# A two-layer hybrid decoder trunk on one core: low halves of weights by adding DMAs, value product with values stationary, last gate with tokens on partitions

## The chip, the core and the metric

The program runs on one core of one Trainium2 chip. A core has five engines that run side by side, each with its own queue of instructions in program order: TensorE (PE, matmuls; its weight loads are listed as PEld and overlap the matmuls), VectorE (DVE), ScalarE (ACT), GpSimd (POOL) and SyncE (SP), which here only issues DMAs. Sixteen DMA engines move data. Matmul results land in PSUM (eight banks of 128 partitions x 512 floats); everything else works in SBUF. The metric is the device time in microseconds of one execution, lower is better; it is the median of three runs.

## The reference

```python
h = x                                              # (1, 256, 1024)
for i in range(2):
    n = rmsnorm(h, norm_g[i])
    z = n @ w_in[i] + b_in[i]                      # 1024 -> 3652 columns
    (c_val, c_glu, c_gate, p_in, p_gate, q, k, v, a_gate, qi, ki, wi) = split(z)
    ya = conv_module(c_val, c_glu, ...) * silu(c_gate)          # 31 taps, layernorm, silu, 256x256
    yb = pool_mixer(p_in, ...) * silu(p_gate)                   # windows 2, 4, 8, 16
    q, k, qi, ki = rope(q), rope(k), rope(qi), rope(ki)
    # per query: the 64 best causal keys by the indexer's score, softmax over them, 8 heads of 64
    yc = sparse_attention(q, k, v, qi, ki, wi) * silu(a_gate)
    h = h + concat([ya, yb, yc]) @ w_out[i]        # 1024 x 1024
    h = h + (p[i] @ ple_w[i]) * sigmoid(h @ ple_gate_w[i])      # 256 x 1024, 1024 x 1024
return rmsnorm(h, final_norm_g)
```

## The kernel before, in words

All activations lie transposed: channels on partitions, the 256 tokens along the free axis (`h` is 128 x 8 x 256). Every large product is made of three products of rounded halves. A weight is cut into `hi`, its rounding to fp32r, and `lo` = weight - `hi`, an activation likewise (`xhi`, `xlo`, or `yhi`, `ylo`); `mm3` adds hi*xhi, hi*xlo and lo*xhi in PSUM, each a matmul of 128 x 128 weights with 256 columns. Small products (scores, value product, transposes) are plain fp32, which the trace lists as two matmul records each, transposes as one.

`chunk` brings in 1 MB of weights (128 x 2048) by a DMA from SP into one of three `raw` buffers and cuts it in two halves of 128 x 1024. For each, `copy` on ACT (L255) makes `hi`, and `sub_hi` makes `lo` on DVE (L275) or POOL (L277), whichever is free first in the recorded order. There are six `hi` and six `lo` buffers, so three chunks' worth. A half feeds 24 matmuls, a chunk 48.

A layer goes: norm factors; `gemm_in` for the projection in chunks of 256 columns (numbered, `C_VAL` = 0 to `QI` = 13), rotary by `rope_pair` with SBUF-to-SBUF DMAs (`zs<-z`) and multiplies on POOL or DVE; the indexer's scores and the choice of 64 keys (DVE); attention for query half t = 1, then 0; convolution, layernorm and pooling (mostly DVE and POOL, spread beside the projections); `gemm_out("out")`, residual add, `gemm_out("gate")`, sigmoid, multiply by `ple` = p @ ple_w, add. In the attention, `lg` (queries on partitions) is transposed to `pTs`, and the value product takes `pTs` as the stationary side and 64 columns of `vt` as the moving side, into `bank 7` with queries on partitions. The result is scaled by `rinv` into `oT` (tile `q4`) and later transposed back (`f,q` in the trace).

At the end of the second layer, `gemm_out("gate")` finishes the 8 column blocks in parts, the last two of one block each. Then come the sums of squares by matmuls with `ones` (`norm_scale`), the power -0.5 on POOL (`rsqrt`), two transposes that spread the factor over the partitions, and five multiplies on DVE, each followed by an output DMA.

The order is not that of the code. Every operation is recorded in `Order` with costs and dependencies, and `issue` writes all of them out, engine by engine, by rank: the length of the path behind an operation plus a number from the table `FIRST` for its tag. So the table decides what stands behind what on each engine.

Of the kernel before, what the change touches and what calls it, by code (L numbers as in the profile page):

```python
# [48 lines left out]
SP_FG = L * SP_N  # L49
SP_TOT = SP_FG + 8  # L50

RAW, HIL = 3, 6
WARM = 13
OUT_ORDER = (2, 3, 4, 5, 6, 7, 0, 1)
OUT_OUTER, GATE_OUTER = 6, 4

# [71 lines left out]
class Order:  # L128
# [83 lines left out]
    def mm(self, o, lhsT, rhs, start, stop):  # L212
        n, m = rhs.free_size(), lhsT.free_size()
        if rhs.dtype == F32:
            occ, flow = 2 * max(112 * m // 128, 833 * n // 1000 + 3), 1667 * n // 1000
            if lhsT.shape[0] <= 64:
                occ = 2 * max(112 * m // 128, 417 * n // 1000 + 3)
# [230 lines left out]
def trunk(ctx: ExitStack, tc: tile.TileContext, xT, pT, w_in, w_ki, w_v, w_out, w_gate, w_ple,  # L448
# [153 lines left out]
    def layer(l, sqs, ple):  # L602
# [360 lines left out]
        for d, n, o in acc:  # L963
            last = l == L - 1 and d == KT - 1
            r = slice(d, d + n)
            if d >= 6 and l == L - 1:
                sums.append(ring("g", 1, (128, 2, S))[:, d - 6:d - 5])
# [135 lines left out]
```

## Time and profile before

| what | value |
|---|---|
| median of three runs | 337.77 us (336.79 to 339.85) |
| the profiled execution | 337.35 us, of which the span from first to last instruction is 335.6 us |
| busy share PE, PEld, DVE, ACT, POOL | 94%, 91%, 78%, 55%, 34% |
| granted TensorE clock | full speed (2.4 GHz) from the warm-up until the tail |
| moved by DMA | 56.80 MB, mean 169 GB/s |

The busy share of PE is counted from overlapping matmuls, so it says little about spare room; the distance between the starts of neighbouring matmuls says more. The chain of the work that ended last belongs to PE for 54% of the span.

### The profile page before, as it was taken

How to read it: one execution, taken by the hardware profiler on the slowest of the kernel's cores; microseconds unless marked ns; L12 is line 12 of the kernel's file. 1: busy time of each engine (PE TensorE's matmuls, PEld its weight loads, DVE VectorE, ACT ScalarE, POOL GpSimd, SP SyncE). 2: the span in 40 equal slices, each digit the busy share in tenths (PEclk: the TensorE clock that was granted, in tenths of full speed). 3: DMA queues.
4: the chain of work that ended last, by engine and by line, in shares of the span. 5: the costliest groups of instructions: out<-in, count | busy, mean ns of one | idle time of the engine just before them, and what ended most of it. 6: DMA issues, size and time to landing. Idle time of an engine off the chain costs nothing.

```text
span 335.6 us, 6643 instructions
## 1 busy us (share of the span) xinstructions
PE 317.0 (94%) x2575; PEld 304.9 (91%) x2575; DVE 263.0 (78%) x566; ACT 185.0 (55%) x318; POOL 115.7 (34%) x106
## 2 busy tenths in 40 slices
PE   7799999889999999999999999989999999999991
PEld 3799999888899899999999999989889999999980
DVE  2987989899896847685696989999998962777573
ACT  3757553571657944565486635446775871647340
POOL 2004156588789600001101207697766000002000
PEclk9999999999999999999999999999999999999996
DMA  7997394532655082637237547275451641370003
GB/s 203 350 352 303 82 374 158 168 147 49 237 200 208 2 297 95 250 107 226 111 94 250 193 149 273 65 259 161 147 173 80 251 169 83 127 250 2 2 0 125
DMA packets 13406, 56.80 MB, mean 169 GB/s; under 512 B 2112, under 2 KB 3264, under 8 KB 7872
## 3 DMA queue, kind: packets, MB, share of 16 engines
q1 hardware_dynamic: 13088, 56.00, 47.8%
q8 instruction: 20, 0.33, 0.4%
q10 hardware_dynamic: 288, 0.39, 0.3%
q14 instruction: 10, 0.08, 0.1%
HBM read 51.93 MB, written 1.05 MB: 158 GB/s over the span
## 4 chain that ended last, share of the span: by engine, by line
PE 54%; DVE 14%; DMA 13%; ACT 8%; POOL 4%; issue 3%; SPq 2%; POOLq 0%; DVEq 0%; ACTq 0%
PE bank L221 51%; DMA raw<-in_w_in_dram 7%; DVE lo L275 4%; DMA zs<-z 4%; ACT hi L255 4%; PE bank L225 3%; SPq L307 2%; DMA raw<-in_w_ple_dram 2%; POOL zrk L267 2%; DVE bank L282 2%; DVE bank L265 1%; POOL zs L267 1%; ACT z L230 1%; ACT bank L230 1%; DVE xlo L275 1%
## 5 line engine op out<-in xcount | busy, mean ns | idle before, releaser
L221 PE MATMUL bank<-xhi,hi 128*128 128x256 f32 x528 | 150.8, 287 | 1.1 <-DVE f L282 0.6
L221 PE MATMUL bank<-xlo,hi 128*128 128x256 f32 (+1 forms) x528 | 147.3, 281 | 0.0
L221 PE MATMUL bank<-xhi,lo 128*128 128x256 f32 x512 | 143.9, 281 | 2.1 <-POOL lo L277 1.1
L255 ACT ACTIVATE hi<-raw 128x1024 fp32r<-128x1024 f32 (+2 forms) x95 | 93.9, 1015 | 61.0 <-PE bank L221 29.2
L275 DVE TENSOR_TENSOR lo<-raw,hi 128x1024 fp32r<-128x1024 f32 (+2 forms) x79 | 91.8, 1184 | 28.7 <-ACT hi L255 27.8
L221 PEld LDWEIGHTS bank<-xhi,hi 128*128 128x128 f32 x528 | 99.5, 189 | 2.6 <-DVE f L282 0.8
L221 PEld LDWEIGHTS bank<-xhi,lo 128*128 128x128 f32 x512 | 96.7, 189 | 2.7 <-DVE lo L275 1.4
L221 PEld LDWEIGHTS bank<-xlo,hi 128*128 128x128 f32 (+1 forms) x528 | 98.6, 187 | 0.1
L282 DVE SCALAR_TENSOR_TENSOR bank<-f,f,bank 128x256 f32<-128x256 f32 x116 | 56.0, 483 | 1.6
L277 POOL TENSOR_TENSOR lo<-raw,hi 128x1024 fp32r<-128x1024 f32 (+1 forms) x19 | 45.4, 2400 | 30.2 <-DVE lo L275 11.8
L221 PE MATMUL bank<-yhi,hi 128*128 128x256 f32 x128 | 36.2, 283 | 0.0
L221 PE MATMUL bank<-yhi,lo 128*128 128x256 f32 x128 | 35.9, 281 | 0.0
L221 PE MATMUL bank<-ylo,hi 128*128 128x256 f32 x128 | 35.9, 280 | 0.0
L277 POOL TENSOR_TENSOR xlo<-f,xhi 128x256 fp32r<-128x256 f32 x4 | 3.6, 924 | 73.2 <-ACT xhi L255 36.7
L221 PEld LDWEIGHTS bank<-yhi,hi 128*128 128x128 f32 x128 | 24.1, 188 | 0.1
L221 PEld LDWEIGHTS bank<-ylo,hi 128*128 128x128 f32 x128 | 24.1, 188 | 0.0
L221 PEld LDWEIGHTS bank<-yhi,lo 128*128 128x128 f32 x128 | 24.1, 188 | 0.0
L267 POOL TENSOR_TENSOR acc<-acc 128x256 f32<-128x256 f32 x3 | 2.2, 742 | 55.7 <-DVE acc L265 35.8
L265 DVE TENSOR_TENSOR bank<-bank,rb 128x512 f32<-128x512 f32 (+1 forms) x26 | 17.3, 672 | 3.8 <-PE bank L221 2.8
L221 PE MATMUL bank<-hi,xhi 128*128 128x260 f32 (+1 forms) x64 | 18.3, 286 | 0.0
L230 ACT ACTIVATE lg<-lg,nmax 128x256 f32<-128x256 f32 (+1 forms) x32 | 14.2, 448 | 7.1 <-DVE nmax L800 7.1
L221 PE MATMUL bank<-lo,xhi 128*128 128x260 f32 (+1 forms) x64 | 18.1, 283 | 0.0
(139 smaller groups left out, 480.3 us busy)
## 6 DMA issues: line engine op xcount, KB each, us to landing
raw<-in_w_in_dram SPq DMA_DIRECT2D x25, 1024.0 KB, 5.4
raw<-in_w_out_dram SPq DMA_DIRECT2D x8, 1024.0 KB, 4.8
raw<-in_w_gate_dram SPq DMA_DIRECT2D x8, 1024.0 KB, 4.8
zs<-z SPq DMA_DIRECT2D x40, 64.0 KB, 3.0
raw<-in_w_v_dram SPq DMA_DIRECT2D x2, 1040.0 KB, 5.6
raw<-in_w_ple_dram SPq DMA_DIRECT2D x8, 256.0 KB, 3.9
raw<-in_w_in_dram SPq DMA_DIRECT2D x4, 256.0 KB, 5.9
f<-in_xT_dram SPq DMA_DIRECT2D x4, 256.0 KB, 5.7
```

The lines of the kernel that those rows point to most:

```text
L221: lambda: self.nc.tensor.matmul(o, lhsT, rhs, start=start, stop=stop, skip_group_check=True))],
L225: self.add([("pe", 195, 109, None, lambda: self.nc.tensor.transpose(o, i, ident))], [i, ident], [o])
L230: self.add([self.on_act(o, i, lambda: self.nc.scalar.activation(o, i, func, bias=bias, scale=scale, **kw), len(ptr), self.TABLE.get(func), ...
L255: ways.append(self.on_act(o, i, lambda: self.nc.scalar.activation(o, i, AF.Copy)))
L265: ways.append(self.on_dve(n, lambda: self.nc.vector.tensor_tensor(o, a, b, op), late=late))
L267: ways.append(self.on_pool(n, lambda: self.nc.gpsimd.tensor_tensor(o, a, b, op)))
L275: ways.append(self.on_dve(n, lambda: self.nc.vector.tensor_tensor(o, a, hb, OP.subtract), late=late))
L277: ways.append(self.on_pool(n, lambda: self.nc.gpsimd.tensor_tensor(o, a, hb, OP.subtract)))
L282: self.add([self.on_dve(o.free_size(), lambda: self.nc.vector.scalar_tensor_tensor(o, a, s, b, op0=op0, op1=op1), len(ptr))], [a, b] + ptr ...
L307: self.add([("dma", nbytes, 590 if inner else 440, None, lambda: q.dma_start(o, i))], [i] if i.space != bass.MemoryType.DRAM else [], [o] ...
```

## The change

Four things change, and the table `FIRST` is another one throughout.

1. For seven of the projection's chunks (`SUMS`: Q1, K0, K1, V1, A0, A1, P_GATE), both halves, both layers, so 28 halves, `lo` is no longer a subtraction. ACT writes -`hi` into `lo` (`neg`), and a DMA issued by POOL adds `raw` to it in place (`plus`).
2. In the value product, `vt` (64 columns of one head) is stationary and `pTs` moves with 128 columns. The two heads of a pair write partitions 0 to 63 and 64 to 127 of bank 7, so the result is transposed already. The factors `rinv` are spread by ACT into a 128 x 512 tile `ons`, transposed four times, copied, and multiplied in. The later transposes of `oT` go.
3. In the last layer, the gate and ple products have tokens on partitions: the activations are stationary and the weights move with 512 columns (256 in the last two parts, see `LAST_PARTS`). `h` is transposed for it (`ht`, 16 transposes).
4. The final norm then works along the free axis: ACT squares with a sum (`ssq`), DVE folds the sums into `nv`, POOL takes the power, ACT and DVE scale. The final norm's weights come in as a 128 x 1024 tile `gb` (0.5 MB more to load). No matmul is left behind the last gate matmul. The output is written token by token.

```diff
+SUMS = {f"{a} {c} {l}" for a in range(2) for c in (Q1, K0, K1, V1, A0, A1, P_GATE) for l in range(L)}
+LAST_PARTS = ((0, 0, 512), (0, 512, 512), (1, 0, 512), (1, 512, 256), (1, 768, 256))
 FIRST = {
-    "at00 0": 144188, "at00 1": -27913, "at04 1": 2080, "at10 0": 181, "at10 1": -2016, "at12 0": 3776,
+    "at00 0": -341946, "at04 0": 78573, "at04 1": 97213, "at10 0": -120473, "at10 1": -75424, "at12 0": 24407,
...
+    def neg(self, o, i):
+        self.add([self.on_act(o, i, lambda: self.nc.scalar.activation(o, i.bitcast(F32), AF.Copy, scale=-1.0))], [i], [o])
+
+    def plus(self, o, i):
+
+        self.add([("pool", self.SUM_WAY, self.SUM_NEXT, None,
+                   lambda: self.nc.gpsimd.dma_start(o, i, accum_op=OP.add))], [i, o], [o])
...
                 with R.part(f"s{a // n} {tag}"):
+                    if f"{a // n} {tag}" in SUMS:
+                        R.copy(hi[:, :n], raw[:, a:a + n], "act")
+                        R.neg(lo[:, :n], hi[:, :n])
+                        R.plus(lo[:, :n], raw[:, a:a + n])
+                        continue
...
-                    for i in range(nh):
-                        hh = 2 * (g0 + i) + e
-                        for kt in range(t + 1):
-                            j = i * (t + 1) + kt
-                            R.mm(po[:, (c0 + i) * 64:(c0 + i + 1) * 64], pTs[:, j * 128:(j + 1) * 128],
-                                 vt[:, kt, hh * 64:(hh + 1) * 64], start=(g0 == 0 and e == 0 and j == 0), stop=(kt == t))
+                    held[e] = pTs
+                for i in range(nh):
+                    f = g0 + i
+                    for kt in range(t + 1):
+                        j = i * (t + 1) + kt
+                        for e in range(2):
+                            R.mm(po[64 * e:64 * e + 64, f * 128:(f + 1) * 128], vt[:, kt, (2 * f + e) * 64:(2 * f + e + 1) * 64],
+                                 held[e][:, j * 128:(j + 1) * 128], start=(f == 0 and kt == 0), stop=(kt == t))
...
+        for i, part in enumerate(order):
...
+                    xh, xl = hhi[:, k, t * 128:(t + 1) * 128], hlo[:, k, t * 128:(t + 1) * 128]
+                    with R.bundle():
+                        R.mm(o, xh, hi[:, c:c + n], start=(k == 0), stop=False)
+                        R.mm(o, xh, lo[:, c:c + n], start=False, stop=False)
+                        R.mm(o, xl, hi[:, c:c + n], start=False, stop=(k == KT - 1))
...
+            R.act(o, o, AF.Sigmoid)
+            R.tt(o, o, ple[:, t, r], OP.mult)
+            R.tt(ht[t][:, r], o, ht[t][:, r], OP.add)
...
+            R.act(junk[:, :n], ht[t][:, r], AF.Square, accum=ssq[:, t, nth:nth + 1])
+            R.tt(hg[t][:, r], ht[t][:, r], gb[:, r], OP.mult, "dve" if end else "dve pool")
...
+                R.stt(v, s1, 1.0 / D, v, OP.mult, OP.add)
+            if end:
+                y = ring(f"nyr{t}", 1, (128, 1))
+                R.pool(750, [v, mhalf], [y], lambda v=v, y=y: nc.gpsimd.tensor_tensor(y, v, mhalf[:, :1], OP.pow))
...
+                    R.scaled(o, o, y)
+                    R.dma(out[t * 128:(t + 1) * 128, c:c + n], o, n << 9, "sp" if q % 2 == 0 else "act")
```

How the instructions stand, at three places. The first is PE in the second layer's attention for t = 1, at the first value products; `vt,pTs` and `pTs,vt` are the value product, `f,lg` the transposes, `zrk,zrq` the scores. Before:

```order
L221 MATMUL bank7_68<-vt45_125,pTs59_139 128x64
L221 MATMUL bank4_65<-zrk54_134,zrq53_133 128x256 x2
L221 MATMUL bank5_66<-zrk54_134,zrq53_133 128x256 x2
L225 MATMUL bank6_67<-f0_69,lg12_92 128x128 x4
L221 MATMUL bank7_68<-vt45_125,pTs59_139 128x64 x3
```

And now, in the same layer:

```order
L226 MATMUL bank6_67<-f0_69,lg12_92 128x128 x4
L222 MATMUL bank7_68<-pTs59_139,vt45_125 64x128
L222 MATMUL bank4_65<-zrk54_134,zrq53_133 128x128 x4
L222 MATMUL bank7_68<-pTs60_140,vt45_125 64x128
L222 MATMUL bank7_68<-pTs59_139,vt45_125 64x128
L222 MATMUL bank7_68<-pTs60_140,vt45_125 64x128
L222 MATMUL bank7_68<-pTs59_139,vt45_125 64x128
L222 MATMUL bank7_68<-pTs60_140,vt45_125 64x128
L222 MATMUL bank7_68<-pTs59_139,vt45_125 64x128
L222 MATMUL bank7_68<-pTs60_140,vt45_125 64x128
```

The products of the two heads of a pair now alternate, in one run of seven and a single one ahead of it; there are six such runs and six single ones in the program.

The second place is POOL in the second layer, where the projections of keys, values and gates are under way; `zrq`, `zrk` and `zs` are rotary work, `lo` the low halves. Before:

```order
L267 TENSOR_TENSOR zrq53_133<-zrq53_133,zs39_119 128x512
L267 TENSOR_TENSOR zrk54_134<-zrk54_134,zs38_118 128x512
L277 TENSOR_TENSOR lo29_109<-raw16_96,hi19_99 128x1024
L267 TENSOR_TENSOR zrk54_134<-zrk54_134,zs39_119 128x512
L277 TENSOR_TENSOR lo26_106<-raw15_95,hi22_102 128x1024
L267 TENSOR_TENSOR pen052_132<-pen052_132,f4_79 128x128
L277 TENSOR_TENSOR lo27_107<-raw15_95,hi23_103 128x1024
```

And now:

```order
L287 DMA lo28_108<-raw16_96 128x1024
L287 DMA lo29_109<-raw16_96 128x1024
L268 TENSOR_TENSOR zrq53_133<-zrq53_133,zs39_119 128x512
L268 TENSOR_TENSOR zrk54_134<-z37_117,f4_79 128x512
L287 DMA lo24_104<-raw17_97 128x1024
L268 TENSOR_TENSOR zrk54_134<-zrk54_134,zs39_119 128x512
L278 TENSOR_TENSOR lo27_107<-raw15_95,hi23_103 128x1024
L268 TENSOR_TENSOR pen052_132<-pen052_132,f4_79 128x128
L287 DMA lo28_108<-raw16_96 128x1024
L287 DMA lo25_105<-raw17_97 128x1024
L287 DMA lo29_109<-raw16_96 128x1024
```

Adding DMAs stand between the rotary multiplies where subtractions stood, and there are more of them.

The third place is the end of PE's queue. Before, from the last gate matmul:

```order
L221 MATMUL bank_68<-xhi_114,lo_105 128x256
L221 MATMUL bank_65<-f_74,acc_111 128x1 x2
L221 MATMUL bank_65<-f_74,g_123 128x1 x4
L225 MATMUL bank_66<-f_69,nyr_121 128x128 x2
```

And now, from the last but one part of the gate:

```order
L222 MATMUL bank_63<-hi_101,xlo_115 128x256
L226 MATMUL bank_66<-f_69,f_80 128x128 x4
L226 MATMUL bank_62<-f_69,f_80 128x128 x4
L222 MATMUL bank_63<-hi_98,xhi_114 128x256
L222 MATMUL bank_63<-lo_108,xhi_114 128x256
L222 MATMUL bank_63<-hi_98,xlo_115 128x256
```

The sums and spreads behind the last gate matmul are gone; eight of the transposes of `h` stand ahead of the last part.

## Rows read from the trace of the kernel before

**Rows 1.** Stretches: length; busy PE, PEld, DVE, ACT, POOL; clock, DMA share, GB/s.
```profile
37.00:115.00 78.00, 74.63 (x610) 71.44 (x610) 68.50 (x192) 43.30 (x87) 53.60 (x43) 1.00 0.49 172
...
200.00:272.60 72.60, 70.64 (x581) 67.63 (x580) 67.66 (x184) 45.31 (x90) 43.57 (x38) 1.00 0.52 179
...
321.30:335.60 14.30, 6.45 (x50) 5.74 (x48) 7.69 (x19) 2.73 (x8) 1.44 (x2) 0.79 0.20 73
```

**Rows 2.** Chain that ended last, in order of time: start, length, what; one piece.
```profile
272.62 48.63 PE bank L221 x404
```

**Rows 3.** Waits of PE: who waited for whom; total us, times, longest.
```profile
PE bank L221 <- DVE lo L275: 1.4, 4, 0.5
...
PE bank L221 <- POOL lo L277: 1.1, 1, 1.1
```

**Rows 4.** Timeline of PE: start, length of the group, line, operands, count.
```profile
112.81 1.03 PE L221 MATMUL bank<-pd,mt 128*128 128x256 f32 x4
...
254.97 1.67 PE L221 MATMUL bank<-vt,pTs 128*128 128x64 f32 x14
256.48 0.61 PE L225 MATMUL bank<-f,lg 128*128 128x128 f32 x4
```

**Rows 5.** Weight loads by shape: busy us, mean ns; idle before.
```profile
L221 PEld LDWEIGHTS bank<-zrk,zrq 64*128 64x128 f32 x64 | 7.5, 186 | 3.7 <-POOL zrk L267 2.5 <-issue 0.2
...
L221 PEld LDWEIGHTS bank<-xlo,hi 128*64 128x64 f32 x16 | 2.1, 134 | 0.0
```

**Rows 6.** Timeline of PE around tiles of 64 columns and of 64 rows.
```profile
187.77 0.28 PE L221 MATMUL bank<-xlo,hi 128*64 128x256 f32 x1
187.88 0.28 PE L221 MATMUL bank<-xhi,hi 128*128 128x256 f32 x1
...
243.96 0.71 PE L221 MATMUL bank<-zrk,zrq 64*128 64x128 f32 x4
244.60 0.44 PE L225 MATMUL bank<-f,lg 128*128 128x128 f32 x2
```

**Rows 7.** Groups off PE: busy us, mean ns; idle before them and its ends.
```profile
L255 ACT ACTIVATE hi<-raw 128x1024 fp32r<-128x1024 f32 x82 | 84.3, 1055 | 50.7 <-PE bank L221 28.4 <-DMA raw<-in_w_in_dram 12.0 <-POOL qir L267 6.2
L275 DVE TENSOR_TENSOR lo<-raw,hi 128x1024 fp32r<-128x1024 f32 x64 | 79.2, 1262 | 22.2 <-ACT hi L255 21.4 <-PE bank L221 0.5
...
L277 POOL TENSOR_TENSOR lo<-raw,hi 128x1024 fp32r<-128x1024 f32 x18 | 44.1, 2461 | 23.2 <-DVE lo L275 11.8 <-ACT hi L255 8.5 <-DVE zrk L265 2.2
...
L230 ACT ACTIVATION_READ_ACCUMULATOR lg<-lg,nmax 128x1 f32 x32 | 6.1, 190 | 0.0
```

**Rows 8.** DMA: the main queue's share; issues, KB each, us to landing.
```profile
q1 hardware_dynamic: 13088, 56.00, 47.8%
...
raw<-in_w_in_dram SPq DMA_DIRECT2D x25, 1024.0 KB, 5.4
...
zs<-z SPq DMA_DIRECT2D x40, 64.0 KB, 3.0
```

**Rows 9.** Timeline of the tail, all engines.
```profile
323.95 0.36 ACT L230 ACTIVATE bank<-bank 128x256 f32<-128x256 f32 x1
...
324.69 0.43 DVE L265 TENSOR_TENSOR bank<-bank,ple 128x256 f32<-128x256 f32 x1
...
325.22 0.28 PE L221 MATMUL bank<-xhi,lo 128*128 128x256 f32 x1
...
325.86 0.42 ACT L248 ACTIVATE g<-f 128x256 f32<-128x256 f32 x1
...
326.88 0.35 DVE L294 TENSOR_SCALAR ag<-f,f 128x256 f32<-128x256 f32 x1
...
327.89 0.16 DVE L288 TENSOR_SCALAR nv<-bank 128x2 f32<-128x2 f32 x1 [0.65 <-PE bank L221]
328.13 0.70 POOL L547 TENSOR_TENSOR nyr<-nv,f 128x2 f32<-128x2 f32 x1 [2.54 <-DVE nv L288]
...
331.92 0.33 SPq L307 DMA_DIRECT2D out_dram<-ag  x1
```

More of the change, by code (lines that the diff above doesn't have):

```diff
@@ L325 @@
     VECTOR_PAUSE, POOL_LATE = 30, -500
+    SUM_WAY, SUM_NEXT = 5500, 1100
     def issue(self):
@@ L577, in ple_gemm @@
         w = chunk(f"ple {l}", w_ple[l], pieces=4, late=0 if l == 0 else VECTOR_LATE)
+        if l == L - 1:
+            ple = ring("ple", 1, (128, KT, S)).rearrange("p (t a) s -> p t (a s)", t=2)
+            for a in range(2):
+                hi, lo = (x[:, :1024].rearrange("p (b k n) -> p k b n", b=2, k=2) for x in w[a])
+                for t in range(2):
+                    pb = bank()
+                    o = pb.rearrange("p (b n) -> p b n", b=2)
+                    R.tag = f"g ple{2 * a + t} {l}"
+                    with R.grouped():
+                        for k in range(2):
+                            with R.bundle():
+                                c0 = k * S + t * 128
+                                xh, xl = phi[:, c0:c0 + 128], plo[:, c0:c0 + 128]
+                                R.mm(o, xh, hi[:, k], start=(k == 0), stop=False)
+                                R.mm(o, xh, lo[:, k], start=False, stop=False)
+                                R.mm(o, xl, hi[:, k], start=False, stop=(k == 1))
+                    R.copy(ple[:, t, a * 512:(a + 1) * 512], pb, "act dve")
+            return ple
         ple = ring("ple", 1, (128, KT, S))
@@ L960, in layer @@
             R.sub_hi(hlo[:, r, :], h[:, r, :], hhi[:, r, :], "dve pool")
+        if l == L - 1:
+            return last_gate(hhi, hlo, ple, [banks[3], bank("att"), bank("att"), bank()])
         acc = gemm_out("gate", w_gate, hhi, hlo)
-        sums = [ring("acc", 1, (128, 2, S))]
+        sums = ring("acc", 1, (128, 2, S))
         for d, n, o in acc:
-            last = l == L - 1 and d == KT - 1
             r = slice(d, d + n)
-            if d >= 6 and l == L - 1:
-                sums.append(ring("g", 1, (128, 2, S))[:, d - 6:d - 5])
-            for c in range(0, S, S // 2 if last else S):
-                t = slice(c, c + S // 2 if last else c + S)
-                R.tag = f"o{d} {l}"
-                s = o[:, :, t]
-                if last:
-                    if c == 0:
-                        sl = ring("lg", 2, (128, 512))
-                    s = sl[:, t].unsqueeze(1)
-                R.act(s, o[:, :, t], AF.Sigmoid)
-                R.tt(s, s, ple[:, r, t], OP.mult)
-                R.tt(h[:, r, t], s, h[:, r, t], OP.add)
-                R.tag = f"sq{d} {l}"
-                if d >= 6 and l == L - 1:
-                    R.sq(sums[-1][:, :, t], h[:, r, t])
-                elif d == 7:
-                    square(sums[0], 6)
-                elif d < 6:
-                    square(sums[0], d)
@@ L986, in layer @@
-        R.tag = f"sum {l}"
-        R.tt(sums[0][:, :1], sums[0][:, :1], sums[0][:, 1:], OP.add, "dve pool")
-        sums[0] = sums[0][:, :1]
-        return sums
+            R.tag = f"o{d} {l}"
+            R.act(o, o, AF.Sigmoid)
+            R.tt(o, o, ple[:, r, :], OP.mult)
+            R.tt(h[:, r, :], o, h[:, r, :], OP.add)
+            R.tag = f"sq{d} {l}"
+            if d == 7:
+                square(sums, 6)
+            elif d < 6:
+                square(sums, d)
+        R.tag = f"sum {l}"
@@ new lines, in layer, with last_gate @@
+        R.tt(sums[:, :1], sums[:, :1], sums[:, 1:], OP.add, "dve pool")
+        return (sums[:, :1],)
+    def last_gate(hhi, hlo, ple, accs):
+        l = L - 1
+        gb = ring("zrq", 1, (128, 4, S)).rearrange("p a s -> p (a s)")
+        R.tag = "gb"
+        R.dma(gb, fg, 1 << 19)
+        ht = [ring("zrk", 1, (128, 4, S)).rearrange("p a s -> p (a s)"),
+              ring("vt", 1, (128, 2, 512)).rearrange("p a s -> p (a s)")]
+        for a in range(2):
+            for t in range(2):
+                R.tag = f"ht{a}{t}"
+                tb = bank("acc" if a == 0 else "att")
+                for j in range(4):
+                    R.tr(tb[:, j * 128:(j + 1) * 128], h[:, 4 * a + j, t * 128:(t + 1) * 128], ident)
+                R.copy(ht[t][:, a * 512:(a + 1) * 512], tb, "act dve")
+        hg = [ring("q4", 1, (128, 4, S)).rearrange("p a s -> p (a s)"),
+              ring("ag", 1, (128, 4, S)).rearrange("p a s -> p (a s)")]
+        ssq = ring("ssq", 1, (128, 2, 4))
+        junk = ring("pTs", 2, (128, 512))
+        w = {}
+        halves = ((0, 512), (512, 512))
+        order = [[(k, t, c, n) for k in range(GATE_OUTER) for t in range(2) for c, n in halves]]
+        order += [[(k, t, c, n) for k in range(GATE_OUTER, KT)] for t, c, n in LAST_PARTS]
+        for i, part in enumerate(order):
+            with R.grouped():
+                for k, t, c, n in part:
+                    if k not in w:
+                        k0 = k // 2 * 2
+                        w[k0], w[k0 + 1] = chunk(f"gate{k // 2} {l}", w_gate[l, k // 2])
+                    R.tag = f"g gate{i} {l}"
+                    hi, lo = w[k]
+                    o = accs[2 * t + c // 512][:, c % 512:c % 512 + n]
+                    xh, xl = hhi[:, k, t * 128:(t + 1) * 128], hlo[:, k, t * 128:(t + 1) * 128]
+                    with R.bundle():
+                        R.mm(o, xh, hi[:, c:c + n], start=(k == 0), stop=False)
+                        R.mm(o, xh, lo[:, c:c + n], start=False, stop=False)
+                        R.mm(o, xl, hi[:, c:c + n], start=False, stop=(k == KT - 1))
+            if i == 0:
+                continue
+            t, c, n = LAST_PARTS[i - 1]
+            o, r = accs[2 * t + c // 512][:, c % 512:c % 512 + n], slice(c, c + n)
+            R.tag = f"o{i}"
+            R.act(o, o, AF.Sigmoid)
+            R.tt(o, o, ple[:, t, r], OP.mult)
+            R.tt(ht[t][:, r], o, ht[t][:, r], OP.add)
+            R.tag = f"sq{i}"
+            nth = [x for x in LAST_PARTS if x[0] == t].index((t, c, n))
+            end = t != ([x[0] for x in LAST_PARTS] + [-1])[i]
+            R.act(junk[:, :n], ht[t][:, r], AF.Square, accum=ssq[:, t, nth:nth + 1])
+            R.tt(hg[t][:, r], ht[t][:, r], gb[:, r], OP.mult, "dve" if end else "dve pool")
+            R.tag = f"norm{t}"
+            v = ring(f"nv{t}", 1, (128, 1))
+            s1 = ssq[:, t, nth:nth + 1]
+            if nth == 0:
+                R.ts(v, s1, 1.0 / D, EPS, OP.mult, OP.add)
+            else:
+                R.stt(v, s1, 1.0 / D, v, OP.mult, OP.add)
+            if end:
+                y = ring(f"nyr{t}", 1, (128, 1))
+                R.pool(750, [v, mhalf], [y], lambda v=v, y=y: nc.gpsimd.tensor_tensor(y, v, mhalf[:, :1], OP.pow))
+                for q, (c, n) in enumerate(((0, 512), (512, 512)) if t == 0 else ((0, 512), (512, 256), (768, 256))):
+                    R.tag = f"end{t}{q}"
+                    o = hg[t][:, c:c + n]
+                    R.scaled(o, o, y)
+                    R.dma(out[t * 128:(t + 1) * 128, c:c + n], o, n << 9, "sp" if q % 2 == 0 else "act")
@@ L1002, in trunk @@
             ple = ple_gemm(l + 1)
-    R.tag = "hg"
-    hg = [ring("q4", 1), ring("ag", 1)]
-    for k in range(KT):
-        o, i, g = hg[k // 4][:, k % 4], h[:, k, :], spt[:, SP_FG + k:SP_FG + k + 1]
-        R.scaled(o, i, g)
-    R.tag = "end"
-    _, rb = norm_scale(*sqs)
-    k = 0
-    for i, n in enumerate((1, 1, 2, 2, 2)):
-        o = hg[k // 4][:, k % 4:k % 4 + n]
-        R.tag = f"end{i}"
-        R.tt(o, o, rb[:, :S].unsqueeze(1).to_broadcast([128, n, S]), OP.mult)
-        R.dma(out[:, k:k + n, :], o, n << 17, "sp" if i % 2 == 0 else "act")
-        k += n
     R.issue()
```

38 lines of the change are left out of this document (20 added, 18 removed), and 113 rows, old and new, of the table FIRST.

## The prediction

> **What bounds the kernel now.** I read the stretches first, for the share of each engine by time, then the chain that ended last, then the waits of PE and its timeline, and last the tail.
>
> In the gate of the second layer the chain is one piece of PE work, 404 matmuls in 48.63 us [rows 2]: 0.120 us from one to the next, with no wait. That is the pitch of a 128 x 128 by 256 matmul, and the chain shows a second such run of 434 matmuls from 115 us. In the two stretches of projections and attention the reader is to compare counts with lengths: 610 records at 0.120 are 73.2 of 78 us, 581 are 69.7 of 72.6 [rows 1]. So outside the first 37 us (loads and warm-up) and the tail PE loses about 7.7 us, and only work taken from PE, its small gaps, and the tail can pay. DVE is busy for 68.50 of 78 and 67.66 of 72.6 us there [rows 1], yet PE's waits for low halves come to 1.4 us for DVE and 1.1 us for POOL in the whole run [rows 3]. Relief of DVE alone is worth no more than that.
>
> In the tail the last gate matmul starts at 325.22 and runs 0.28 us; the last output DMA is issued at 331.92 [rows 9]. These 6.4 us hold arithmetic on short data, and after them come a landing and the end of the program, which stay.
>
> **Value product.** It was 48 matmuls, 96 records in the trace. Fourteen of them stand between 254.97 and 256.48 [rows 4]: 0.108 us each, 10.4 us in all. They moved 64 columns and loaded 128, so the load sets this. Now 64 columns are loaded: a load of 64 takes 134 ns against 186 for 128 columns [rows 5], 0.052 less, so a load-bound pitch falls to about 0.056. The moving side has 128 columns. Four fp32 records of 256 columns span 1.03 us, the last one about 0.38 of it: 0.217 each [rows 4], so 128 columns take 0.108 if the two heads follow each other and 0.054 each if they run side by side in the two column halves of the array. No row shows two such halves side by side. The bounds are 96 x 0.108 = 10.4 us (no gain) and 96 x 0.056 = 5.4 us (5.0 gained). I take the second less 0.5 us for the twelve places where a matmul has no partner next to it (six runs, each with one sent ahead): **-4.5 us**. The array's side-by-side use for the scores, 64 rows each, is in this kernel already, and it is the nearest row.
>
> The transposes of `oT` (16) go and 16 of `ons` come, at equal price. Eight ACT copies of 128 x 512 come in; ACT is busy 43.30 of 78 and 45.31 of 72.6 us [rows 1], and the last two stand before the second half of the output product, behind other projections that PE has to do. I cost them at nothing; without that cover each half's chain would be about 2 us longer.
>
> **Gate and ple of the last layer.** The gate was 192 matmuls at 0.120 = 23.0 us [rows 2]. Now it is 84 with 512 columns and 24 with 256. No row has 512 columns at full clock in this type. A 256-column fp32 record occupies the array as long as I expect of 512 columns here, so I take 0.217 [rows 4]: 18.2 + 2.9 = 21.1, **-1.9 us**. The other end is twice 0.120, no gain. The same for ple: 48 x 0.120 = 5.8 becomes 24 x 0.217 = 5.2, **-0.6 us**. The 16 transposes of `h` cost 0.11 each, as (0.61 - 0.28) / 3 for `f,lg` [rows 4]: **+1.8 us**. The 0.5 MB of norm weights ride on SP before the output weights, in a time when only half of the DMA engines' time is used; nothing.
>
> **Tail.** From the end of the last matmul: sigmoid 0.36, multiply 0.43, add 0.43, square 0.42 and the reading of its sum 0.19 [rows 7, 9], fold 0.16, power 0.70, scaling of 512 columns about 0.6 (256 take 0.35 [rows 9]), scaling of 256 another 0.35. That is 3.64; seven hand-offs at about 0.05, as between the sigmoid's and the multiply's neighbours, make 4.0. It was 6.4: **-2.4 us**, with -1.5 and -3.2 as ends for hand-offs of 0.2 or a last scaling that runs beside the first. The removed scalings by the norm weights and squares were off PE's path.
>
> **Low halves.** Counted in the order, DVE makes 49 instead of 64 halves of 1024 columns and POOL 5 instead of 18: 15 x 1.262 = 18.9 us off DVE, 13 x 2.461 = 32 off POOL [rows 7]. ACT gets 28 x 1.055 = 29.5 us, about 15 in each stretch, which makes 58 of 78 and 60 of 72.6. POOL must issue 28 DMAs, and between rotary multiplies: what is queued behind an issue that waits for ACT is `zrq` and `zrk`, and the scores on PE wait for those. An issue on SP takes a few tenths of a us; on POOL no row shows it, and its upper bound is the subtraction that it replaces.
>
> The path of a half gets longer: `hi` 1.06, `-hi` 1.06, then the add, of T us to landing. Two covers hide it. The first are the `lo` buffers: a buffer is free five halves before it is needed, 5 x 24 x 0.120 = 14.4 us, and ACT's rounding indeed waits 28.4 us for PE to free buffers [rows 7]. The second are the three raw buffers: load 5.4 [rows 8], four ACT passes 4.2, then T, within the 17.3 us in which PE eats three chunks (144 x 0.120). So T may be up to 7.7 us. Half a megabyte lands between 3.0 us (64 KB inside SBUF) and 5.4 us (1 MB), and reading the destination too at most doubles the upper one: 3.0 to 10.8 [rows 8]. I take 5, since the moved bytes are between those rows and only part of a landing time is transfer. Then the cover holds, and the adds cost nothing. The sixteen engines: 56 MB took 47.8% of 335.6 us, 2.9 us per MB [rows 8], so an add takes 1.4 to 2.9 us of them and fourteen 20 to 41 us in a stretch where 38 of 78 (38 of 72.6) are taken [rows 1]. Full at the upper end, free at the lower.
>
> With DVE relieved and a new order I give PE's waits **-1 us**, from -2.5 (all of its waits for low halves [rows 3]) to what the second rival says.
>
> **Sum.** -4.5 - 1.9 - 0.6 + 1.8 - 2.4 - 1.0 = -8.6. The profiled execution took 337.35 us, 1.75 more than its span; 337.35 - 8.6 = 328.75, and the median is 0.4 above that execution: **329**.
>
> **Rivals.** First, the column halves don't pair, or changing the array's shape costs. For 64-row tiles it does: four scores of 128 columns take from 243.96 to 244.60, 0.64 us for 4 x 0.108, so about 0.2 us a visit [rows 6]. For 64-column tiles the trace shows none: such a matmul at 187.77 has its neighbour of 128 columns 0.11 us behind it [rows 6]. But those stay in the left half. With twelve visits at 0.25 us the time is 332; without pairing 333.5; with both 336.5. The Trainium skill, "TensorEngine Tiling (Array Packing)", section Key Properties, says that changing the tiling mode drains TensorE, and that different tiles can load weights and multiply in parallel. By its first half the visits would be paid (332), by its second they would pair; the rows of 64 rows agree with the first half, those of 64 columns don't. Chance 0.22.
>
> Second, slower: the adds land late. The mechanism is the raw ring: with T = 10.8 the cycle is 20.4 instead of 17.3 us, 1.0 us lost in each of 14 chunks, 14 us, and the gain of waits gone: 344. It decides from T = 9.8, where 14 chunks lose 9.6 us and the change is worth nothing. Against it speaks that ACT waits for PE and not PE for ACT [rows 7]; for it, that the DMA engines can run full. Chance 0.13.
>
> Third, the new order closes gaps that the old one left: of the 7.7 us in the two stretches 4 more go. 325. For it: DVE, which stands nearest to its limit there, loses a seventh of the work. Against: PE waits for it for 1.4 us only. Chance 0.12. That the change does only part of what it says (the gate at no gain) lies in the range of the forecast, 331.
>
> **How the numbers follow.** The forecast has 0.53. Its own range is 325.5 to 332. The range to 8 in 10 leaves out most of the late adds and the best of the third rival: 322.5 to 338. One per cent is 3.4 us, about what a measurement of this kernel can tell from no change (three runs lay 336.79 to 339.85). Faster than 334.4: nearly all of 0.53, 0.12 of the first rival's 0.22, 0.12, so 0.76. Slower than 341.1: most of the late adds, 0.10. Between: 0.14.
>
> **What would show it.** In the trace of the changed kernel: records of the value product 0.055 apart in pairs (right) or 0.108 (first rival); gaps of 0.1 us where 64 and 128 columns meet; gate matmuls of 512 columns 0.217 apart; adds landing in 5 us or near 10; PE waiting for a DMA on `lo`, which would be new; the last output DMA 4 us behind the last matmul. The prediction is wrong above all if the adds' landing under load passes 8 us, or if POOL's issues hold up the rotary work so that scores come late.

## The result, and the profile after

The changed kernel takes 369.86 us (median of 4 runs, 369.09 to 371.02), the kernel before 337.39 us on the same chip: 1.095 times as long, 95% interval 1.089 to 1.100. The forecast was 329.0 us in a range of 322.5 to 338.0. It was wrong in direction, and by 41 us. Some executions of a kernel run at a lower granted clock and take longer; the times below leave them out, so two of them (338.1 and 342.5 us) stand a little under what the recorded expectations call 338.4 and 343.

From the page of the changed kernel: busy us, share and count of each engine; TensorE's clock and the DMA engines' share in 40 slices; then two DMA queues with packets, MB and share of the sixteen engines' span.

```profile
PE 328.4 (89%) x2469; PEld 304.7 (83%) x2469; DVE 247.9 (67%) x548; ACT 215.6 (59%) x357; POOL 108.6 (30%) x121
...
PEclk9999998798999999999999999897899899999998
DMA  6991899995953972745336598988749736372011
...
q1 hardware_dynamic: 13232, 56.52, 43.7%
q0 software_dynamic: 4032, 14.68, 21.2%
```

DVE was relieved as announced. PE has 106 records fewer, yet it is busy longer: the clock fell in places where it had not before. Queue q0 is new: it is the 28 adds, and they hold a fifth of the time of all sixteen DMA engines, on top of what q1 took already [rows 8].

The stretches (columns as in [rows 1]): the two with projections and attention (13 and 11 adds), each followed by one of other products (no add, and one); at the end three short pieces from the first of them.

```profile
46.00:134.00 88.00, 72.43 (x540) 64.93 (x538) 55.90 (x169) 56.88 (x104) 40.91 (x42) 0.94 0.83 211
134.00:183.00 49.00, 48.92 (x408) 48.66 (x409) 32.50 (x43) 23.93 (x35) 2.72 (x3) 1.00 0.51 183
...
220.00:306.00 86.00, 74.20 (x555) 68.27 (x553) 60.46 (x174) 52.83 (x96) 37.99 (x41) 0.92 0.77 213
306.00:357.00 51.00, 50.92 (x343) 46.58 (x343) 28.04 (x35) 25.84 (x40) 6.49 (x6) 1.00 0.32 108
...
46.00:61.00 15.00, 9.69 (x76) 8.87 (x74) 9.34 (x20) 8.34 (x10) 7.42 (x8) 1.00 1.04 227
61.00:68.00 7.00, 3.43 (x16) 3.43 (x16) 3.19 (x7) 4.62 (x6) 5.28 (x5) 0.52 1.06 207
68.00:76.30 8.30, 8.30 (x70) 7.50 (x70) 4.54 (x12) 1.07 (x2) 0.26 (x1) 0.99 1.04 272
```

Where no add or a single one runs, PE is as full as ever. The loss lies in the other two: 540 and 555 records in 88 and 86 us, where before 610 and 581 stood in 78 and 72.6 [rows 1], at a DMA share of 0.83 and 0.77 in place of 0.49 and 0.52. From 46 to 76 us the DMA engines are full without a break (the view shows a share a little above 1). There PE stands still from 58.9 to 64.6 us, and from 61 to 68 us the granted clock is 0.52 of 2.4 GHz in the mean, nearly all of it at the lower level of 1.2 GHz. Over both stretches the clock is 0.94 and 0.92, a loss of 5 + 7 = 12 us at most.

Who waited for whom: PE's waits, then one line each of SP's and ACT's (total us, times, longest).

```profile
PE bank L222 <- DMA lo<-raw: 14.2, 8, 5.7
PE bank L222 <- ACT z L231: 5.2, 2, 2.7
PE bank L222 <- POOL qir L268: 3.3, 1, 3.3
PE bank L222 <- POOL zrk L268: 2.4, 2, 2.1
...
SPq L316 <- DMA lo<-raw: 69.7, 11, 12.1
...
ACT hi L256 <- DMA raw<-in_w_in_dram: 42.6, 14, 7.1
```

PE now waits for the adds themselves, up to 5.7 us, where its longest waits for a low half were 0.5 and 1.1 us [rows 3]. SP, which issues all loads and the rotary staging in one order, waits 69.7 us for adds to free a raw buffer. ACT waits for the weights 42.6 us instead of 12.0 [rows 7]. The landing times go with that (KB each, median us from issue to landing):

```profile
raw<-in_w_in_dram SPq DMA_DIRECT2D x25, 1024.0 KB, 6.6
lo<-raw POOLq DMA_DIRECT2D x28, 512.0 KB, 7.6
...
zs<-z SPq DMA_DIRECT2D x40, 64.0 KB, 5.2
```

The adds land in 7.6 us (4.5 to 11.9). But the weights also went from 5.4 to 6.6 and the 64 KB of the rotary staging from 3.0 to 5.2 [rows 8]. The chain that ended last belongs to PE for about half of the span, as before, but its share of DMA went from 13% to 19%, which is 44 and 70 us. Its shares by engine, here and in the kernel before, then some of its pieces (start, length, what):

```profile
PE 52%; DMA 19%; ACT 8%; DVE 7%; issue 5%; SPq 5%; POOL 3%; POOLq 0%; DVEq 0%; ACTq 0%
...
PE 54%; DVE 14%; DMA 13%; ACT 8%; POOL 4%; issue 3%; SPq 2%; POOLq 0%; DVEq 0%; ACTq 0%
...
56.06 6.35 DMA zs<-z
73.42 8.06 DMA zs<-z
87.95 8.59 DMA lo<-raw
...
134.08 49.11 PE bank L222 x408
...
222.57 4.50 DMA lo<-raw
...
274.57 11.79 DMA lo<-raw
```

By their shares of the chain the adds have 25 us of it and the rotary staging 21 (14 before). The projection's weights have 15, less than the 24 of before: they land later, but the chain runs through other things.

Last, the timeline: one wait for an add, a short and a long run of the value product, the 512-column matmuls of the gate, the transposes of `h`, and the tail.

```profile
64.57 0.58 PE L222 MATMUL bank<-xhi,lo 128*128 128x256 f32 x1 [5.67 <-DMA lo<-raw]
...
101.77 0.43 PE L222 MATMUL bank<-pTs,vt 128*64 128x128 f32 x2
102.14 0.44 PE L226 MATMUL bank<-f,lg 128*128 128x128 f32 x2
...
105.36 1.09 PE L222 MATMUL bank<-pTs,vt 128*64 128x128 f32 x14
106.38 0.44 PE L226 MATMUL bank<-f,lg 128*128 128x128 f32 x2
...
352.23 0.39 PE L222 MATMUL bank<-hi,xlo 128*128 128x512 f32 x1
352.46 0.40 PE L222 MATMUL bank<-hi,xhi 128*128 128x512 f32 x1
...
356.65 1.03 PE L226 MATMUL bank<-f,f 128*128 128x128 f32 x8
358.40 0.39 PE L222 MATMUL bank<-hi,xhi 128*128 128x256 f32 x1 [0.71 <-DVE vt L266]
...
359.80 0.28 PE L222 MATMUL bank<-hi,xlo 128*128 128x256 f32 x1
...
363.38 0.81 SPq L316 DMA_DIRECT2D out_dram<-ag  x2
363.65 0.37 ACTq L316 DMA_DIRECT2D out_dram<-ag  x1
```

The value product has six runs of 14 records and six of 2. A run of 2 holds PE for 0.37 us, one of 14 for 1.02. So a record costs (1.02 - 0.37) / 12 = 0.054 us, and each visit 0.26 us more: 8.3 us in all. The 512-column matmuls stand 0.232 us apart. From the end of the last matmul (360.08) to the last issue are 3.6 us.

### The profile page after: what moved, and what is told of

Its sections match the earlier page's. It is cut to its first block, busy times and chain, and to the rows that moved or that the text cites. A ratio compares the mean times of both kernels' runs of the same rounds, so it can differ in the third digit from the quotient of the medians.

```text
span 367.6 us, 6520 instructions
## 1 busy us (share of the span) xinstructions
PE 328.4 (89%) x2469; PEld 304.7 (83%) x2469; DVE 247.9 (67%) x548; ACT 215.6 (59%) x357; POOL 108.6 (30%) x121
## 3 DMA queue, kind: packets, MB, share of 16 engines
q0 software_dynamic: 4032, 14.68, 21.2%
## 4 chain that ended last, share of the span: by engine, by line
PE 52%; DMA 19%; ACT 8%; DVE 7%; issue 5%; SPq 5%; POOL 3%; POOLq 0%; DVEq 0%; ACTq 0%
PE bank L222 50%; DMA lo<-raw 7%; DMA zs<-z 6%; SPq L316 5%; DMA raw<-in_w_in_dram 4%; ACT hi L256 2%; DVE lo L276 2%; PE bank L226 2%; ACT lo L282 2%; DMA f<-in_xT_dram 2%; DVE bank L266 1%; DMA raw<-in_w_ple_dram 1%; POOL zs L268 1%; ACT c L231 1%; POOL zrq L268 1%
## 5 line engine op out<-in xcount | busy, mean ns | idle before, releaser
L222 PE MATMUL bank<-xhi,lo 128*128 128x256 f32 x448 | 129.6, 289 | 14.9 <-DMA lo<-raw 14.2
L256 ACT ACTIVATE hi<-raw 128x1024 fp32r<-128x1024 f32 (+2 forms) x95 | 94.1, 1014 | 76.2 <-DMA raw<-in_w_in_dram 42.6
L222 PE MATMUL bank<-xhi,hi 128*128 128x256 f32 x464 | 136.2, 296 | 2.5 <-ACT z L231 2.5
L222 PE MATMUL bank<-xlo,hi 128*128 128x256 f32 (+1 forms) x464 | 132.4, 287 | 0.4 <-DVE xlo L276 0.4
L222 PEld LDWEIGHTS bank<-xhi,lo 128*128 128x128 f32 x448 | 87.8, 196 | 16.7 <-DMA lo<-raw 15.9
L276 DVE TENSOR_TENSOR lo<-raw,hi 128x1024 fp32r<-128x1024 f32 (+2 forms) x64 | 72.5, 1155 | 14.4 <-ACT hi L256 14.2
L287 POOL DMA_DIRECT2D lo<-raw x28 | 25.5, 934 | 35.1 <-ACT lo L282 28.6
L222 PE MATMUL bank<-hi,xhi 128*128 128x256 f32 (+2 forms) x100 | 32.4, 324 | 3.4 <-ACT z L231 2.7
L222 PE MATMUL bank<-hi,xlo 128*128 128x256 f32 (+2 forms) x100 | 32.0, 320 | 0.0
L222 PE MATMUL bank<-lo,xhi 128*128 128x256 f32 (+2 forms) x100 | 32.0, 320 | 0.0
L282 ACT ACTIVATE lo<-hi 128x1024 fp32r<-128x1024 f32 x28 | 29.0, 1051 | 0.3
L222 PEld LDWEIGHTS bank<-yhi,hi 128*128 128x128 f32 x128 | 24.1, 188 | 1.6 <-DVE ylo L276 1.6
L222 PEld LDWEIGHTS bank<-ylo,hi 128*128 128x128 f32 x128 | 24.1, 188 | 0.0
L222 PEld LDWEIGHTS bank<-yhi,lo 128*128 128x128 f32 x128 | 24.1, 188 | 0.0
```

Source lines behind the costliest of these rows:

```text
L222: lambda: self.nc.tensor.matmul(o, lhsT, rhs, start=start, stop=stop, skip_group_check=True))],
L256: ways.append(self.on_act(o, i, lambda: self.nc.scalar.activation(o, i, AF.Copy)))
L276: ways.append(self.on_dve(n, lambda: self.nc.vector.tensor_tensor(o, a, hb, OP.subtract), late=late))
L282: self.add([self.on_act(o, i, lambda: self.nc.scalar.activation(o, i.bitcast(F32), AF.Copy, scale=-1.0))], [i], [o])
L287: lambda: self.nc.gpsimd.dma_start(o, i, accum_op=OP.add))], [i, o], [o])
```

## The experiments

In theory A the adds cost the loss: their bytes fill the DMA engines, so that low halves, weights and rotary operands all land late. Theory B blames the rest: the new order, or the other three parts. Within A, it is open whether PE merely waits for long adds or whether everything that shares the engines is late.

**Adds of 128 columns.** The order is the changed kernel's, instruction by instruction; the other 896 columns of those low halves stay -`hi`.

```diff
-  self.nc.gpsimd.dma_start(o, i, accum_op=OP.add)
+  self.nc.gpsimd.dma_start(o[:, :128], i[:, :128], accum_op=OP.add)
```

> The changed kernel in its own order, but each adding DMA moves 128 of the 1024 columns (the other 896 columns of lo keep -hi, so the output is not the reference's). POOL still issues 28 DMAs behind the same waits. Theory A (the adds land too late and fill the DMA engines; they took 7.6 us to landing and 21.2% of the sixteen engines): the landing falls to 2 to 4 us, PE no longer waits for lo, the clock stays up, 328 to 335 us. Theory B (the new order, the 28 more ACT passes or POOL's issues between the rotary multiplies hold up PE, not the landing): 360 us or more. Theory C (the adds' load on the engines delays weights and rotary copies, their landing itself matters little): this run can't tell it from A.

341.2 us, 1.014 times before (1.007 to 1.021), between the two recorded windows and much nearer to that of theory A. Landings in this run, then two pieces of its chain:

```profile
raw<-in_w_in_dram SPq DMA_DIRECT2D x25, 1024.0 KB, 5.4
...
zs<-z SPq DMA_DIRECT2D x40, 64.0 KB, 2.6
...
lo<-raw POOLq DMA_DIRECT2D x28, 64.0 KB, 3.4
```

```profile
119.13 66.93 PE bank L222 x542
...
277.06 26.56 PE bank L222 x215
```

The second piece (215 matmuls) starts at 306.30 in the changed kernel: 29.2 us are lost before it, 15.0 of them before the first piece (134.08 there). So all 28.7 us between the two kernels hang on the adds' bytes, since order and instruction counts are the same. Up to some 12 of them go with the clock: the same 2469 PE records are busy for 316.7 us here, at full clock but for the end, and for 328.4 in the changed kernel. Beside before the small adds still lose 4.8 us (336.4 on that chip).

**A copy in place of the add.** Same bytes written, the destination not read; `lo` is then `raw`.

```diff
-  self.nc.gpsimd.dma_start(o, i, accum_op=OP.add)
+  self.nc.gpsimd.dma_start(o, i)
```

> The changed kernel in its own order, but POOL's 28 DMAs copy raw into lo without adding (lo is then raw, so the output is not the reference's): same bytes written, same queue, the destination is not read. Theory A in the form that the second read is what costs: engine time of the 28 falls from 78 us to about 40 (1.4 us each), landing to 4 to 6 us, 335 to 345 us. Theory A in the form that any half megabyte on this queue lands late: landing stays at 7 us or more, 360 us or more. Theory B: 365 or more, whatever the landing.

355.0 us, 1.054 times (1.047 to 1.060), in none of the three recorded windows: half of the loss stays, at a share of 12.3% for q0 in place of 21.2%. (POOL's issue of a copy also takes less, 0.59 us against 0.88.)

**Load that nobody waits for, and its control.** The adds move 128 columns; behind each, a second add goes to DRAM, with 896 columns, or with 32 in the control.

```diff
+  room = nc.dram_tensor("room", (28, 128, 896), F32, kind="Internal").ap()     # control: 32
-  self.nc.gpsimd.dma_start(o, i, accum_op=OP.add)
+  self.nc.gpsimd.dma_start(o[:, :128], i[:, :128], accum_op=OP.add)
+  nc.gpsimd.dma_start(room[next(at)], ct[:, :896], accum_op=OP.add)            # control: :32
```

> The adds move 128 of 1024 columns (the rest of each low half stays minus the high half), and behind each a second add moves the other 896 columns of a constant tile to a buffer in DRAM that nobody reads or waits for. The transfer work stays, the low halves need not wait for it. If the busy DMA engines are the cost (weights, rotary operands and low halves alike land late behind the adds' bytes): 357 to 371 us. If the cost is that the matmuls wait for a low half whose own add is long: at most 349 us, near the 341 of the small adds alone.

> As the kernel with a second add to DRAM beside each small add, but the second one moves 32 columns, so GpSimd issues just as often and the DMA engines carry next to nothing more than with the small adds alone. If the 28 us that the second adds of 896 columns cost were their bytes on the DMA engines: 341 to 350 us. If they were GpSimd's issuing (28 x 1.4 us more on its queue, behind which the rotary work waits): 360 to 370.

368.9 us with 896 columns, 345.7 with 32, both in the windows recorded for the adds' bytes as the cost. The control is 4.5 us above the small adds alone: its 28 more issues take 1.2 us of POOL each, and its q0 has 11 us more of the sixteen engines. The other 23.2 us come with bytes that no instruction waits for. PE's waits with 896 columns, then one of SP's:

```profile
PE bank L222 <- POOL qir L268: 8.3, 2, 5.3
PE bank L222 <- DMA lo<-raw: 6.2, 2, 4.2
PE bank L222 <- POOL zrk L268: 5.5, 2, 4.7
...
SPq L316 <- DMA lo<-raw: 61.7, 12, 10.1
```

PE waits less for low halves (6.2 against 14.2 us), and the time is about the same: the rotary results `qir` and `zrk`, whose operands come by `zs<-z`, are late instead. Together (the engines' time is q0's share of the span; the landings and waits with 32 columns are from an execution of 351.3 us):

| kernel (same order) | q0 share, us | us to landing: add, `zs`, weights | SP's waits for adds, us | time |
|---|---|---|---|---|
| adds of 128 columns | 4.7%, 16 | 3.4, 2.6, 5.4 | 30.4 | 341.2 |
| and 32 columns beside | 7.7%, 27 | 4.1, 3.1, 5.3 | 41.8 | 345.7 |
| copies | 12.3%, 43 | 5.2, 4.6, 6.1 | 49.3 | 355.0 |
| the changed kernel | 21.2%, 78 | 7.6, 5.2, 6.6 | 69.7 | 369.9 |
| 128 columns, and 896 beside | 24.1%, 88 | 5.7, 4.5, 6.0 | 61.7 | 368.9 |

The time goes with the load on the engines. Some 62 us more of their time cost 28.7 us where the low halves wait for it (first row to fourth) and 23.2 where no instruction waits for the added bytes (second to last): about four fifths of the loss need no matmul that waits for its own long add. One thing these runs leave open. The small adds stand behind the large ones in q0 and land late themselves (5.7 against 4.1 us), so SP waits longer for raw buffers in the run with 896 columns too, and all loads and rotary staging queue behind these waits. How much is slow transfers and how much is SP held up was not separated. (The load beside also goes to DRAM, where the change's adds stay in SBUF.) Slow transfers are a part of it, since a landing counts from its own issue: the `zs<-z` landings have 6.6% of that run's chain (24 us) and 4.2% of the control's (15). (The kernel before lay between 336.4 and 337.7 us beside all runs of this section.)

**Adds planned late.** All adds, the order made anew with their landing put 4 us later (`SUM_WAY` 9500); the planned price of the new value product goes up as in the last experiments below.

```diff
-    SUM_WAY, SUM_NEXT = 5500, 1100
+    SUM_WAY, SUM_NEXT = 9500, 1000
```

> The changed kernel with all 28 adds, the order made anew with the add's landing put at 9.5 us in place of 5.5. If the adds cost only because they land later than the order allows for: 330 to 342 us. If their bytes on the DMA engines are the cost (weights, rotary operands and low halves late together, which no earlier start of the add mends): 350 to 370 us.

364.8 us, 1.082 times (1.075 to 1.089). PE's waits:

```profile
PE bank L224 <- DVE qir L268: 9.2, 2, 6.3
PE bank L224 <- POOL zrk L270: 7.3, 1, 7.3
PE bank L224 <- ACT z L233: 5.3, 1, 5.3
PE bank L224 <- DMA lo<-raw: 1.9, 2, 1.3
```

The waits for adds are nearly gone (1.9 of 14.2 us), as an earlier start should do. The rotary waits took their place, the weights land in 7.1 us, and 5 us were won. So this order doesn't mend the load on the engines; that no order does is not shown by one.

**Subtractions in the same order.** VectorE makes the 28 halves where the adds were issued.

```diff
-  self.nc.gpsimd.dma_start(o, i, accum_op=OP.add)
+  self.nc.vector.tensor_tensor(o, i, hi.bitcast(F32), OP.subtract)             # neg() issues nothing
```

> The order of the changed kernel, but each of the 28 low halves is made by one VectorE subtraction at the place where the add was issued; ScalarE's negative copy is gone too. VectorE gets 28 x 1.2 us = 34 us more. Theory A (the adds cost the 33 us: late low halves and full DMA engines): 330 to 342 us, the time of the kernel before or of the adds of 128 columns (341), and the weights' loads land in about 5.5 us again. Theory B (the new order or the other three parts cost it): above 352 us, since all of these stay.

362.5 us, which falls in the window of theory B. But the run with small adds has the same order and the same other parts at 341.2, so B can't be what loses the time there. The weights land in 5.1 us and `zs<-z` in 2.0, as theory A says for a run without adds. PE's waits tell what it is:

```profile
PE bank L222 <- POOL qir L268: 7.0, 2, 6.1
PE bank L222 <- DVE vt L303: 4.5, 1, 4.5
PE bank L222 <- POOL zrk L268: 4.4, 3, 2.0
PE bank L222 <- DVE nmax L834: 4.2, 3, 3.3
```

36.7 us were put into VectorE's queue where the order had none, and what stood behind them came late (VectorE has 31% of the chain, 7% in the changed kernel). It doesn't isolate the adds.

**No adds, and the value product alone, under the old tables.** The first is the changed kernel with `SUMS = set()`, the second the kernel before with part 2 put in; each keeps the table `FIRST` of its origin.

> The change without part 1: all low halves by subtraction on DVE or POOL, the other three parts and the table of the changed kernel stay, though that table was made for the adds. Theory A: 328 to 340 us, no waits for DMA on lo. Theory B in the form that the table or parts 2 to 4 lose the time: over 350 us.

> The kernel before with part 2 alone (vt stationary, two heads in two column halves), with the table of before. By the trace of the changed kernel the 96 records take 8.3 instead of 10.4 us: 335 us if that is all, 332 if halves pair fully here, up to 341 if the old table suits the longer chain (spread, transposes, copies) badly. It tells whether part 2 is a gain by itself.

387.8 and 387.1 us: slower than either kernel and far outside what theory A and the part's rows gave. In both, a table made for one set of operations runs another, and both lose about 50 us, so neither tells a part's worth. From here on each set of operations has a table of its own.

**The parts under their own orders.** The edits are `SUMS = set()` (three parts), that and the old value product (last gate, ple and norm alone), part 2 alone, and none (control); each with a new `FIRST`. The second orders leave more time between a DMA's landing, or a VectorE result, and what waits for it than the first ones do. Where the new value product is in, the planned price of its matmuls goes up by 38 ns.

> The changed kernel without any adding DMA: all low halves by subtraction, value product, last gate and norm as changed, and a table of order made anew for these operations. If the adds are what makes the change slow, and the other three parts are worth what their rows in the changed kernel show (value product -2.1, gate and ple -0.6, transposes +1.75, tail -2.6 us): 334 us, between 330 and 338. If the other parts need the adds' relief of VectorE, or cost by themselves: 341 to 355.

> The kernel before with the last gate, ple and norm alone changed and its own table of order: -0.6 + 1.75 - 2.6 = -1.5 us by the rows, 336 us, between 332 and 340. Against the run with the value product also changed it shows what that product is worth in a place of its own: 2 us by its rows; none if its scale transposes and copies take it back.

> The changed kernel without adds, as in the run that took 349.7 us, under a second table of order that leaves more time between a DMA's landing, or a VectorE result, and what waits for it. If that run's loss came from its order (the chain went through VectorE's low halves and convolution taps): 331 to 338 us. If it came from the value product and its extra copies and transposes: 344 us or more again.

> The last gate, ple and norm alone, under a second table made in the same way. The part's own rows give -1.5 us: 333 to 338 us. Against the run with the value product as well: 2 us slower if that product is worth its rows.

> Control: the kernel before, not one operation changed, under a table of order made in the same way as for the two others. If the three parts are worth what their rows say, this is 1.5 us slower than the last gate alone and 3.5 us slower than the three parts: 334 to 339 us. If it is as fast as they are, what they win is the order's.

> The kernel before with the value product alone changed (no adds, last gate and norm as before), under a table of order made for it like that of the unchanged control. If the product is worth its rows (8.3 us in place of 10.4): 2 us less than the control's 338.4, 334 to 338 us. If it is what makes the three parts slow (343 us in the better of two orders): 341 us or more.

> Value product, last gate and norm as changed, no adds, under a third order, found from the one under which the value product alone took 335.9 us. If the parts add up: -2.1 us for the product and -1.3 for the last gate with its tail, about 334 us, 331 to 336, faster than both kernels. If the last gate's transposes and the wait in front of its last part eat what its shorter tail wins (its two runs alone were level): 335 to 337.

> The same operations under a fourth order, to tell how much of any difference is the order's: within 2 us of the third if the parts decide, 5 us or more apart if the order does.

| operations, order | time | ratio to before |
|---|---|---|
| unchanged, second | 338.1 | 1.001 (0.997 to 1.005) |
| last gate, ple and norm, first | 338.1 | 1.002 (0.999 to 1.005) |
| last gate, ple and norm, second | 340.3 | 1.007 (1.004 to 1.010) |
| value product, second | 335.9 | 0.994 (0.991 to 0.997) |
| all three, first | 349.7 | 1.035 (1.030 to 1.040) |
| all three, second | 342.5 | 1.014 (1.009 to 1.019) |
| all three, third | 335.2 | 0.994 (0.991 to 0.997) |
| all three, fourth | 334.2 | 0.989 (0.984 to 0.994) |

The value product alone is 2.0 us faster than before, what its rows say, but it has run under one order only. Last gate and norm alone win nothing that can be measured (340.3 is above its recorded window). The same three parts lie between 334.2 and 349.7 us under four orders, so most of what the two slow runs lost was their orders' doing. Their recorded windows would have put 349.7 down to the parts themselves, and 342.5 lies between its two. Third and fourth are 1.0 us apart, which by the recorded rule speaks for the parts; the first two say that the order can do far more. In the first of the four the chain ran more through VectorE's low halves and convolution taps (5% of it each), and PE's longest wait was for a tap:

```profile
PE bank L223 <- DVE bank L292: 3.7, 1, 3.7
```

The third order starts from the one that suited the value product. The fourth, without a single add, beats both kernels: 1.1% faster than before (0.7 to 1.6), 10% faster than the change. It is the best of four orders, and the unchanged kernel had one new order, so what of the 1.1% belongs to the parts isn't shown.

## Why the prediction was wrong

**Low halves: the step that failed.** The working said "I take 5 ... Then the cover holds, and the adds cost nothing". The landing is 7.6 us, up to 11.9. The cover was reckoned to hold to 7.7, with the weights landing in 5.4 us as before; they took 6.6, and with that the same sum gives 17.3 - 6.6 - 4.2 = 6.5, less than the adds' 7.6. The same paragraph had the number that decided: "an add takes 1.4 to 2.9 us" of the sixteen engines, "full at the upper end". The runs show 21.2% of 367.6 us / 28 = 2.8 us, the upper end, and the engines full from 46 to 76 us. The term that failed is this load, put at nothing: the bytes of the adds cost 28.7 us against the small adds. The forecast took the middle of a landing time and forgot that with this load nothing else keeps its own landing time either. Its sign of being wrong, a landing above 8 us, didn't show in the median of 7.6; its other sign, rotary work that comes late, did, though more by the bytes (23.2 us in the runs with a load beside) than by POOL's issues (at most 4.5).

By the Trainium skill, "DMA: Bandwidth & Descriptors", section Anatomy of one DMA, a DMA issued by GpSimd takes about 2.0 us plus its bytes at 436 GB/s; worked out for 512 KB that is an estimate of 3.2 us. Only the fastest plain copy here came near it, with 2.9 us; the medians are 5.2 for the copy (up to 9.2) and 7.6 for the add, both under load. The same page, Queues, rings and completion order, says that each DMA engine takes turns between the queues, a packet at a time. That fits the 64 KB of `zs<-z`, which land late beside the adds of another queue; no row shows the turns themselves.

**Late adds, the rival given 0.13.** It had the right sign and named half of the mechanism, the raw ring: SP waits 69.7 us for adds, 30.4 with the small ones. Its price (14 us, 344 us at a landing of 10.8) was too small by half, because it let only low halves be late. The load without waiting cost 23.2 us. (Its turning point is a slip too: by its own cycle the change without the gain of waits, -7.6 us, is used up at T = 9.3, not 9.8.) The clock is a part of the loss: behind waits of 2 to 6 us PE ran at 1.2 GHz for a while, which kept it busy about 12 us longer in sum, a term that the prediction didn't have.

**Value product (-4.5).** Mechanism right, size off. Heads pair at 0.054 us a record, as taken (0.056). A visit to the 64-column shape costs 0.26 us, which was the first rival's price (0.25), twelve times; the reading that 64 columns cost no visit, from one such matmul alone, did not carry over. 8.3 us instead of 10.4 is -2.1 us, and the run of that part alone gives -2.0 (-3.1 to -1.0). The Trainium skill's rule, weighed in the prediction ("TensorEngine Tiling (Array Packing)", Key Properties), that changing the tiling mode drains TensorE, agrees with these rows for 64 columns too. Costing the eight copies and the spread factors at nothing fits with that, under this one order.

**Gate (-1.9) and ple (-0.6).** The pitch taken was 0.217, and it is 0.232: 84 x 0.232 + 24 x 0.119 = 22.3 against 23.0 us, and 24 x 0.232 = 5.6 against 5.8. So -0.7 and -0.2. The transposes cost +1.75 as said (16 x 0.109), and 0.71 us of waiting for the copy of `h` in front of the last part, which the working left out. **Tail (-2.4):** 6.4 became 3.6, -2.8. Together parts 3 and 4 are worth -1.2 us by rows; both runs of them alone show no gain, and what takes the rest isn't settled.

**PE's waits (-1).** No gain. DVE went from 78% to 67% and PE didn't notice, as [rows 3] had said: 2.5 us of waits for low halves were all there was to win. The kernel paid 28 adds and 29 us of ACT for them. With the adds nearly free the changed kernel is still at 341.2; with none, under another order, it is at 334.2.

**New order.** Priced as a gain of up to 4 us (the third rival); four orders of the same operations differ by 15 us. The changed kernel's order was planned for adds that land in 5.5 us and load nothing else; with small adds, which come near to that, it runs in 341.2.

## What to carry to other kernels

Before moving work from an engine to DMAs, add up the DMA engines' time in the stretch where they will run, at the upper price, and count every other transfer there as late once the sum nears the stretch. An engine on which the bound one hardly waits is worth no relief, least of all by a queue that carries the bound one's operands. And a part of a change that has its own hand-made or searched order can only be judged under orders made for it, and under more than one: here four differ by 15 us.

## What the runs showed of the hardware

- An accumulating DMA of 512 KB within SBUF took 2.8 us of all sixteen engines, a plain copy of the same size 1.55 (12.3% of 352.5 us / 28): 1.8 times as much.
- With the engines full, 64 KB landed in 7.6 to 9.8 us (60 to 80 us in the changed kernel) against 3.0 before, and SP's issue of it took 1.1 to 1.7 us against a median of 0.59 (longest 1.30) before.
- fp32 matmuls that load 64 columns into alternating halves of the array ran at 0.054 us a record of 128 columns, half of the 0.108 of full width, plus 0.26 us for each visit to that shape.
- Weights of 512 columns in fp32r ran 0.232 us apart, 256 columns 0.119: 1.95 times, so the wide form saves 2.5%.
